# Residual update and transposes at the norm between two blocks, pass order, and a written issue order, in a two-layer decoder trunk

## Chip, cores and metric

The kernel runs on one core of a Trainium2 chip. The metric is the device time of one execution in microseconds (us); three executions of the kernel before gave 572.90, 573.61 and 573.81, with a median of 573.61. One further execution was profiled. All durations below come from it.

## The reference

Two layers act on x (256 tokens by 1024 features, float32). Each layer does:

```
h = rms_norm(x) * g_pre_mix
parts = h @ w_in                      # 1024 x 2840
mix = concat(nsa(parts), fox(parts)) @ w_out
x = x + rms_norm(mix) * g_post_mix
h = rms_norm(x) * g_pre_mlp
y = square(relu(h @ w_up)) @ w_down   # 1024 x 4096, 4096 x 1024
x = x + rms_norm(y) * g_post_mlp
```

`rms_norm(v)` is v times 1/sqrt(mean(v*v) + 1e-6), row by row. The two attention mixers (8 heads each) lie between `w_in` and `w_out`; the change leaves them as they are. What counts here are the three places where one block's result goes through a post-norm into x, and x goes through the next pre-norm into the next block's first product: mixer to MLP in layer 0, MLP of layer 0 to the mixer of layer 1, and mixer to MLP in layer 1. They are called the three junctions below. The end of layer 1 has a post-norm and a store, and no next norm.

## The kernel before

**Data layout.** The 256 tokens are two tiles t = 0, 1 of 128 tokens. Tokens lie on the partitions in `X[t]` (128 x 1024). A product with a weight needs the left operand turned, with features on the partitions: that is `xT`, 8 blocks k of 128 features by 256 tokens.

**High and low parts.** TensorE is used in its fp32r type. Each float32 operand is split into a high part (ScalarE copies it to fp32r: `whi`, `xT[0]`) and a low part (VectorE subtracts the high part from the value: `wlo`, `xT[1]`). A product is then three passes that accumulate in one PSUM bank, in `mm3`: high x high, high x low of the weight, low of x x high of the weight. Some weights get their low part through an accumulating DMA of GpSimd's queue instead, and the products with `w_down` are combined in blocks so that seven products serve for eight; neither is changed.

**A junction.** For token tile t the product leaves two PSUM banks `acc[0]`, `acc[1]` of 512 features. The function `sandwich` does, in three steps separated by `yield`: (1) ScalarE squares both banks with row sums; VectorE multiplies each bank by the product of both gains, `g_post * g_next` (tiles `mg`); seven tiny operations (`rsqrt_sum`) make the factor r of the row; VectorE makes `xg = mg * r + xo` in four pieces of 256, where `xo = x * g_next` was made ahead by `pre_gain`. (2) `to_xT` turns each half of `xg` with four 128 x 128 transposes on TensorE into one PSUM bank, ScalarE makes the high part of 128 x 512 in one instruction and VectorE the low part in one. (3) VectorE multiplies the banks once more, by `g_post` alone (tiles `m`), and adds `m * r` into X in pieces of 512. The row factor of the next norm is not in `xT`: it is applied later, to the next product or through the epsilon of the following norm.

`pre_gain` needs three multiplications of 128 x 1024 per junction, and `load_gains` brings two gain rows, spread over the partitions (512 KB each), into the buffers `gain0` and `gain1`.

**What sets the order.** All operations are first recorded, in the order of the code, by the class `Recorder`; an operation's number is its place in that record (5200 operations). A planner (`order`, `schedule`) then gives each engine its order from costs, due times, a list of overridden ranks (`RANKS`) and a mark `hot` on junction operations (`urgent`). Each engine works through its own instructions in that order: PE (TensorE), DVE (VectorE), ACT (ScalarE), POOL (GpSimd) and SP (SyncE, which issues most of the DMAs). The order between engines is kept only by waits on what an instruction reads and overwrites. Weight loads use nine rotating buffers (`raw`), so a load waits on SP until the splits of the load nine places earlier are done, and everything behind it in SP's queue waits with it.

**What follows a junction.** After the mixer, `up0` forms 512 columns of h @ w_up for t = 0 and then t = 1; after the MLP of layer 0, `in_chunk(0, evac0, by_token=True)` forms 512 columns of h @ w_in, again by tile. Both go through k = 0 to 7 and make all three passes of one k before the next. While the junction of tile 0 is worked on, PE has the products of tile 1 (`out_last`, `down`); while that of tile 1 is worked on, it has the first products of tile 0.

In the profile nearly all lines bear the number L481 (where `emit` issues everything), so operations are told apart by their tiles: `mg`, `m`, `xo`, `gains`, `xT`, `s<-cst,mg` (the transposes of xg, against the identity in `cst`), `pcs` (the scaled scores of the compressed attention branch, split in high and low, transposed against `identr`).

Of the kernel before, what the change touches and what calls it, by code (L numbers as in the profile page):

```python
# [24 lines left out]
P = 128  # L25
D = 1024
S = 256
NT = 2
# [6 lines left out]
LANE = 0.9  # L35
PASSES = 4
LANDING = 3500.0

ADDING, ADDED, CAST = 2600, (5000, 5000), (1870, 2500)
SLACK, LATE = {"vector": 20, "scalar": 20}, 1000  # L40

RAMP = {0: 900, 1: 420}
WAIT = 0.4
WARM = (256, 256, 256, 256, 128)
ENTER, LEAVE = 90, 200
SEQ = [(2, 0), (2, 1), (2, 2), (2, 3), (3, 0), (3, 1), (3, 2), (3, 3)]
EVKEY = 1
FIRSTS = [(k, k + 1) for k in range(8)]
NFIRST = 768
HOLD = 150  # L50
REACH = 40
UPK = 7
TOK, WBUFS, RBUFS = 6, 7, 9
LOAD_LEAD, SPLIT_LEAD, ADD_LEAD, CAST_LEAD = 12, 1, 5, 10
# [11 lines left out]
RANKS = (  # L66
# [17 lines left out]
)  # L84
QT = (1, 1)
# [130 lines left out]
class Op:  # L216
    __slots__ = ("small", "engine", "name", "args", "kw", "key", "urgent", "cost", "deps", "succs", "bufs",
                 "missing", "ready", "start", "end", "tile", "rank")


class Recorder:
    def __init__(self, nc, tc):
        self.nc, self.tc = nc, tc
        self.ops, self.stages, self.fifo, self.key, self.hot, self.lane, self.group = [], [], {}, None, False, None, None
        self.after = None
        for e in ("tensor", "vector", "scalar", "gpsimd", "sync"):
            setattr(self, e, _Engine(self, e))
# [15 lines left out]
    def add(self, engine, name, args, kw):  # L243
        if self.group is not None:
            assert engine == "tensor"
            self.group.append((name, args, kw))
            return
        op = Op()
        op.engine, op.name, op.args, op.kw = engine, name, args, kw
        op.key = len(self.ops) if self.key is None else self.key  # L250
        if self.lane is not None and self.key is None:
            op.key = self.lane + LANE * (len(self.ops) - self.lane)
        op.urgent = self.hot
# [4 lines left out]
        op.tile = _tile(op) if engine == "tensor" else None  # L258
        op.small = engine == "tensor" and not any(v.buf.name.startswith(("whi", "wlo")) for _, v in views)
        op.cost = _cost(op, views) + SLACK.get(engine, 0)  # L260
        deps = {} if self.after is None else {self.after: -1e9}
        op.bufs = []
        for is_out, v in sorted(views, key=lambda x: x[0]):
            b, m = v.buf, v.mask()
            if b not in op.bufs:
                op.bufs.append(b)

            def against(entries):
                for o, p, q, bank in entries:
                    if o is not op and o not in deps and (  # L270
                            (bank and engine == "tensor") or
                            (p[0] < v.p[1] and v.p[0] < p[1] and (m & q).any())):
                        deps[o] = _latency(o, op)

            against(b.writes)
            entry = (op, v.p, m, is_out and b.psum and engine == "tensor")
            if is_out:
                against(b.reads)
                b.writes = [w for w in b.writes if not (
                    w[0] in deps and v.p[0] <= w[1][0] and w[1][1] <= v.p[1] and not (w[2] & ~m).any())]  # L280
                b.writes.append(entry)
            else:
                if b.psum:
                    for o, _, _, _ in b.reads:
                        if o.engine != engine and o is not op and o not in deps:
                            deps[o] = 130.0
                b.reads.append(entry)
        op.deps = deps
        for b in op.bufs:
            if not b.ops:  # L290
                self.fifo.setdefault(b.tag, []).append(b)
            b.ops += 1
        op.succs = []
        for d in deps:
            d.succs.append(op)
        self.ops.append(op)

    def deadlines(self, out):


        due, t = {}, 0.0
        for op in out:
            if op.engine == "tensor":
                due[op], t = t, t + op.cost
        taker = {}
        for q in self.fifo.values():
            for a, b in zip(q, q[q[0].bufs:]):
                taker[a] = b
        first = {}
        for op in out:  # L310
            for b in op.bufs:
                first.setdefault(b, op)
        for op in reversed(out):
            d = due.get(op, t)
            cost = op.cost + LANDING if op.engine == "sync" else op.cost
            for x in op.succs:
                if x.deps[op] > -1e8 and x in due:
                    d = min(d, due[x] - x.deps[op] - cost)
            for b in op.bufs:
                if taker.get(b) in first and first[taker[b]] in due:  # L320
                    d = min(d, due[first[taker[b]]] - (260 if b.psum else 150) - cost)
            due[op] = d
        for op in out:
            op.rank = op.key if op.engine == "tensor" else due[op]

    def order(self):

        for op in self.ops:  # L330
            op.rank = op.key
        done = 0
        for bound in self.stages + [len(self.ops)]:
            rest = self.ops[done:]
            best = None
            for first in ([op.rank for op in rest], [op.key for op in rest]):
                for op, rank in zip(rest, first):
                    op.rank = rank
                for i in range(PASSES + 1):
                    if i:  # L340
                        kept = [op.rank for op in self.ops[:done]]
                        self.deadlines(out)
                        for op, rank in zip(self.ops, kept):
                            op.rank = rank
                    out = self.schedule()
                    end = max(op.end for op in out)
                    if best is None or end < best[0]:
                        best = end, [op.rank for op in rest]
            for op, rank in zip(rest, best[1]):
                op.rank = rank  # L350
            done = bound
# [1513 lines left out]
```

## Time and profile before

| | |
|---|---|
| median of three runs | 573.61 us (572.90 to 573.81) |
| the profiled execution, from first to last instruction | 572.4 us (572.36) |
| PE busy | 564.1 us, 99% of the span, 3696 matmuls |
| DVE busy | 534.5 us, 93% |
| ACT busy | 452.4 us, 79% |
| granted TensorE clock, mean | 0.997 |
| first matmul / last matmul's end | 0.78 us / 566.03 us |

The profiled execution is 1.25 us below the median of the runs; a prediction made against its span is carried over by that difference. "Busy" joins overlapping instructions: matmuls overlap, so a busy PE can still hold short waits of its weight loads (PEld). The stages lie so: attention of layer 0 from 6 to 118 us, its junction to the MLP 118 to 131, the MLP to 281, the junction to layer 1 281 to 300, attention 300 to 400, junction 400 to 414, MLP to 566, and then the last norm and the store.

### The profile page before, as it was taken

Reading aid. Unit: us, or ns where it says so; the run is one execution under the profiler, and the core shown is the slowest. Engines: PE = TensorE matmul, PEld = TensorE weight load, DVE = VectorE, ACT = ScalarE, POOL = GpSimd, SP = SyncE. Lnnn points to the kernel's source line nnn. Section 1 sums busy time; section 2 is a strip of 40 time slices with the busy share of each in tenths; the row PEclk is TensorE's granted clock in tenths of the full one; section 3 lists DMA queues with packets and bytes.
Section 4 is the critical chain, followed back from the end, with each engine's and each line's share of the span. In section 5 each row is a group of like instructions: output and inputs, shape, how many; then the busy total and the mean of one; then the engine's idle time right before and its main releaser. Section 6 shows DMA issues by size and latency. Waiting matters only on the chain.

```text
span 572.4 us, 10587 instructions
## 1 busy us (share of the span) xinstructions
PE 564.1 (99%) x3696; PEld 503.0 (88%) x3696; DVE 534.5 (93%) x1138; ACT 452.4 (79%) x850; POOL 49.4 (9%) x76
## 2 busy tenths in 40 slices
PE   9999999999999999999999999999999999999995
PEld 7988888789999999999889888878899999999994
DVE  7889899989999999999897899997999999999997
ACT  7898888778987877777569969986879877878873
POOL 0000200011010111000000012000111111111000
PEclk9999999999999999999999999999999999999998
DMA  8988737749999899798438685585498989888621
GB/s 322 380 307 288 272 118 237 261 155 275 289 265 289 252 253 318 196 322 229 143 109 289 251 270 156 182 279 192 142 325 238 299 251 279 259 277 257 144 38 74
DMA packets 39430, 135.69 MB, mean 237 GB/s; under 512 B 4657, under 2 KB 4817, under 8 KB 39377
## 3 DMA queue, kind: packets, MB, share of 16 engines
q1 hardware_dynamic: 31456, 106.17, 52.6%
q0 software_dynamic: 7920, 28.84, 23.0%
q8 instruction: 29, 0.48, 0.3%
q14 instruction: 25, 0.20, 0.1%
HBM read 133.92 MB, written 1.07 MB: 236 GB/s over the span
## 4 chain that ended last, share of the span: by engine, by line
PE 93%; DVE 4%; DMA 1%; ACT 1%; issue 0%; DVEq 0%; ACTq 0%
PE s L481 41%; PE acc L481 21%; PE x L481 20%; PE o L481 11%; DMA wraw<-in_w_in_dram 1%; DVE wlo L481 1%; DVE qS L481 0%; DVE m L481 0%; ACT whi L481 0%; DVE pr L481 0%; DVE x L481 0%; DVE rsqrt L481 0%; ACT qT L481 0%; DVE cs L481 0%; DVE gz L481 0%
## 5 line engine op out<-in xcount | busy, mean ns | idle before, releaser
L481 DVE TENSOR_TENSOR wlo<-wraw,whi 128x1024 fp32r<-128x1024 f32 (+2 forms) x156 | 171.9, 1108 | 10.3 <-ACT whi L481 6.2
L481 ACT ACTIVATE whi<-wraw 128x1024 fp32r<-128x1024 f32 (+2 forms) x165 | 157.9, 966 | 27.9 <-PE s L481 15.6
L481 PE MATMUL s<-xT,whi 128*128 128x256 f32 (+1 forms) x832 | 110.0, 283 | 0.0
L481 PEld LDWEIGHTS s<-xT,whi 128*128 128x128 f32 x832 | 105.2, 192 | 4.5 <-ACT y L481 0.3
L481 ACT ACTIVATE whi<-wsum 128x1024 fp32r<-128x1024 f32 x52 | 54.6, 1056 | 14.4 <-DVE wsum L481 6.0
L481 DVE TENSOR_TENSOR wlo<-wsum,whi 128x1024 fp32r<-128x1024 f32 x52 | 63.2, 1221 | 0.7 <-PE s L481 0.4
L481 PE MATMUL s<-xT,wlo 128*128 128x256 f32 x448 | 59.6, 275 | 0.0
L481 PEld LDWEIGHTS s<-xT,wlo 128*128 128x128 f32 x448 | 56.9, 192 | 1.6
L481 PE MATMUL x<-whi,aS 128*128 128x512 f32 x128 | 47.6, 379 | 0.0
L481 ACT ACTIVATE pr<-pr,st 128x256 f32<-128x256 f32 (+1 forms) x96 | 42.8, 450 | 3.7 <-DVE st L481 3.6
L481 PE MATMUL acc<-whi,aS 128*128 128x512 f32 x128 | 44.7, 380 | 0.0
L481 POOL DMA_DIRECT2D wlo<-in_w_up_dram x31 | 26.8, 865 | 150.9 <-ACT wlo L481 108.5
L481 DVE TENSOR_TENSOR wsum<-wraw,wsum 128x512 f32<-128x512 f32 x52 | 35.7, 686 | 0.1
L481 PE MATMUL s<-whi,aS 128*128 128x512 f32 x104 | 35.4, 380 | 0.0
L481 PE MATMUL acc<-whi,xT 128*128 128x512 f32 (+1 forms) x128 | 35.0, 341 | 0.0
L481 PE MATMUL x<-whi,xT 128*128 128x512 f32 x112 | 34.5, 390 | 0.0
L481 ACT ACTIVATE aS<-quads 128x896 fp32r<-128x896 f32 (+3 forms) x31 | 27.5, 891 | 8.7 <-DVE quads L481 8.2
L481 PE MATMUL acc<-xT,whi 128*128 128x512 f32 x128 | 33.0, 386 | 0.0
L481 DVE TENSOR_TENSOR aS<-quads,aS 128x896 fp32r<-128x896 f32 (+3 forms) x31 | 31.5, 1016 | 0.6 <-ACT aS L481 0.5
L481 DVE TENSOR_TENSOR wsum<-wraw 128x1024 f32<-128x1024 f32 x26 | 31.7, 1220 | 0.0
L481 POOL DMA_DIRECT2D whi<-in_w_up_dram x22 | 12.7, 576 | 203.1 <-PE s L481 71.8
L481 DVE TENSOR_TENSOR quads<-quads 128x128 f32<-128x128 f32 (+1 forms) x81 | 26.8, 335 | 1.2 <-ACT quads L481 0.8
(257 smaller groups left out, 1251.5 us busy)
## 6 DMA issues: line engine op xcount, KB each, us to landing
wraw<-in_w_down_dram SPq DMA_DIRECT2D x64, 512.0 KB, 5.7
wraw<-in_w_up_dram SPq DMA_DIRECT2D x42, 512.0 KB, 5.6
wraw<-in_w_in_dram SPq DMA_DIRECT2D x35, 512.0 KB, 5.2
wlo<-in_w_up_dram POOLq DMA_DIRECT2D x31, 512.0 KB, 7.0
whi<-in_w_up_dram POOLq DMA_DIRECT2D x22, 512.0 KB, 5.3
wraw<-in_w_out_dram SPq DMA_DIRECT2D x16, 512.0 KB, 3.7
w<-in_cmp_w_k_dram SPq DMA_DIRECT2D x8, 512.0 KB, 6.1
w<-in_cmp_w_v_dram SPq DMA_DIRECT2D x8, 512.0 KB, 5.6
```

Of the source, the lines that this page charges most:

```text
L481: getattr(getattr(self.nc, op.engine), name)(*[real(v) for v in args], **{k: real(v) for k, v in kw.items()})
```

## The change

Four things are changed, and all three junctions get them.

1. `sandwich` updates X first: `m = acc * g_post`, then `X = m * r + X` in four pieces of 256. `to_xT` turns X itself. `pre_gain`, `xg`, `xo`, the second multiplication by a gain and the later update of X are gone.
2. The next norm's gains are applied after the turn, where features lie on the partitions and a gain is one number per partition. `to_xT` does that inside the split, 128 columns at a time: four ScalarE copies with a scale instead of one of 512, and four VectorE operations `(value * gain) - high` instead of one subtraction of 512. The gains come as 16 more columns in the small `w2` load; the second gain row is not loaded. The step that turns tile t moves behind the update of X.
3. `halves_first`: the first product after a junction makes, for k = 0 to 3, the two passes with the high part of x, then for the same k the pass with its low part, and then the same for k = 4 to 7. The number of matmuls stays.
4. The planner, its costs and `RANKS` are gone. `ISSUE` is a table of the numbers of all 5236 operations (two characters each, to the base of 91) in the order in which they are issued. The table does not hold the planner's order: engine by engine, most operations stand at another place than before, in the attention and MLP stages too.

The record grows by 36: per junction, 16 more operations for the finer splits and updates (8 per tile), one DMA and three multiplications fewer.

```diff
-UPK = 7
+UPK = 14
...
-RANKS = (
...
+ISSUE = (
+    "!,!!!-!#!.!$!%!&!(!)!*#a#v!4!U!5!8!7!9!V!/!W!Z!X$)!+$8!6!Y!^!;!_![!]!0!c!d!f!:!`!a!<!=!e!b!h!k!g!l!i!?!n!>!j!A"
...
+PLACES = "".join(chr(c) for c in range(33, 127) if chr(c) not in "\"\\'")
...
+        n = len(PLACES)
+        issue = [n * PLACES.index(a) + PLACES.index(b) for a, b in zip(ISSUE[::2], ISSUE[1::2])]
+        assert sorted(issue) == list(range(len(self.ops)))
+        return [self.ops[i] for i in issue]
...
-    def load_gains(*rows):
-        g = [None, None]
-        for i, (name, l) in enumerate(rows):
-            g[i] = tile([P, D], F32, name="gains", tag=f"gain{i}")
-            nc.sync.dma_start(g[i], A[name][l].partition_broadcast(P))
+    def load_gain(name, l):
+        g = tile([P, D], F32, name="gains", tag="gain0")
+        nc.sync.dma_start(g, A[name][l].partition_broadcast(P))
         return g
...
-        w2t = small([P, 560], "w2", 1)
-        nc.sync.dma_start(w2t[:, :550], A["w2"][l])
+        w2t = small([P, 568], "w2", 1)
+        nc.sync.dma_start(w2t[:, :566], A["w2"][l])
...
+    def mm3(ps, a, b, start, stop, check=True, passes=(0, 1, 2)):
 
         ps, b = in_turns(ps), [turns(x) for x in b]
-        for j, (u, v) in enumerate(((0, 0), (0, 1), (1, 0))):
+        for j in passes:
+            u, v = ((0, 0), (0, 1), (1, 0))[j]
...
+    def halves_first():
+
+        return [(k, x) for n in (0, 4) for x in ((0, 1), (2,)) for k in range(n, n + 4)]
...
-    def to_xT(t, n, xg, xT):
+    def to_xT(t, n, g, xT):
 
         ps = psum("s")
         with nc.stretch():
             for k in range(4):
-                nc.tensor.transpose(ps[:, k * P:k * P + P], xg[:, k * P:k * P + P], ident)
-        split(ps.rearrange("p (k n) -> p k n", k=4), [y[:, 4 * n:4 * n + 4, t * P:t * P + P] for y in xT[:2]])
-
-    def pre_gain(g_post, g_next):
-
-        xo = []
-        for t in range(NT):
-            xo.append(tile([P, D], F32, name="xo", tag="fT", bufs=2))
-            nc.vector.tensor_mul(xo[t], X[t], g_next)
-        nc.vector.tensor_mul(g_next, g_next, g_post)
-        return g_next, xo
+                nc.tensor.transpose(ps[:, k * P:k * P + P], X[t][:, n * 512 + k * P:n * 512 + k * P + P], ident)
+        into = [[z[:, 4 * n + k, t * P:t * P + P] for z in xT[:2]] for k in range(4)]
+        cols = [(ps[:, k * P:k * P + P], g[:, 4 * n + k:4 * n + k + 1]) for k in range(4)]
+        for (i, c), (hi, _) in zip(cols, into):
+            nc.scalar.activation(hi, i, AF.Copy, scale=c)
+        for (i, c), (hi, lo) in zip(cols, into):
+            nc.vector.scalar_tensor_tensor(lo, i, c, hi.bitcast(F32), op0=OP.mult, op1=OP.subtract)
...
+                for a in (0, 256) if xT else (slice(0, 512),):
+                    a = slice(a, a + 256) if xT else a
+                    x = X[t][:, half(n)][:, a]
+                    nc.vector.scalar_tensor_tensor(x, m[n][:, a], r, x, op0=OP.mult, op1=OP.add)
...
         yield
+        if xT:
+            for n in range(2):
+                to_xT(t, n, g_next, xT)
+            yield
...
+        gains_mlp = par["smT"][:, 38:46]
...
-                    g_post, g_pre2 = load_gains(("g_post_mix", l), ("g_pre_mlp", l))
+                    g_post = load_gain("g_post_mix", l)
...
-        pre = pre_gain(g_post, g_pre2)
...
-            products(0, ps0, UPK, 8)
+            products(0, ps0, UPK, 16)
             square(0, ps0)
-            next(steps[0])
-            next(steps[1])
             ps1 = psum("o")
-            products(1, ps1, 0, 4)
+            products(1, ps1, 0, 8)
             turn(0)
-            products(1, ps1, 4, 8)
+            products(1, ps1, 8, 16)
```

More of the change, by code (lines that the diff above doesn't have):

```diff
@@ L10 @@
-import collections
-import heapq
 from contextlib import ExitStack, contextmanager
@@ L216 @@
 class Op:
-    __slots__ = ("small", "engine", "name", "args", "kw", "key", "urgent", "cost", "deps", "succs", "bufs",
-                 "missing", "ready", "start", "end", "tile", "rank")
+    __slots__ = ("engine", "name", "args", "kw", "bufs")
 class Recorder:
@@ L223, in __init__ @@
         self.nc, self.tc = nc, tc
-        self.ops, self.stages, self.fifo, self.key, self.hot, self.lane, self.group = [], [], {}, None, False, None, None
-        self.after = None
+        self.ops, self.group = [], None
         for e in ("tensor", "vector", "scalar", "gpsimd", "sync"):
@@ L248, in add @@
         op = Op()
[L249 to L253, printed above, removed]
+        op.engine, op.name, op.args, op.kw, op.bufs = engine, name, args, kw, []
         views = []
@@ L257, in add @@
             views += [(i in ("out", "accum_out"), v) for i, v in k.items() if isinstance(v, View)]
[L258 to L295, printed above, removed]
-        self.ops.append(op)
[L298 to L324, printed above, removed]
@@ L326, in order @@
-    def order(self):
[L330 to L351, printed above, removed]
-        for i, rank in RANKS:
-            self.ops[i].rank = rank
-        return self.schedule()
@@ L512, in _product @@
-def _product(name, args, side):
-    n = int(np.prod(args[0].shape[1:]))
-    rounded = args[1].dtype == F32R
-    if rounded and name != "transpose" and args[2].shape[-1] == 2:
-        return max(112.0, n / 2.4 + 3)
-    if name == "transpose":
-        return 85.0 if rounded else 109.0
-    if side > 1:
-        return n / 2.4 + 20 if rounded else n / 0.6 + (60 if n >= 256 else 11)
-    return max(118.0, n / 2.4 + (14 if n > 256 else 13)) if rounded else max(220.0, n / 0.6 + 7)
-def _cost(op, views):
-    out = op.args[0] if op.args else op.kw["out"]
-    n = int(np.prod(out.shape[1:]))
-    part = 100 * (out.shape[0] < P)
-    if op.engine == "gpsimd":
-        return 200 + 0.72 * n + 10 * int(np.prod(out.shape[1:-1]))
-    if op.engine == "sync":
-        v = views[0][1]
-        run = int(np.prod(v.shape[1:])) * 4 * (1.3 if v.buf.name in ("x0", "x1", "bias") else 1.0)
-        return v.shape[0] * run / 360.0
-    if op.engine == "tensor":
-        if op.name == "stretch":
-            side = P // min(op.tile)
-            return sum(_product(*x[:2], side) for x in op.args[2][::side])
-        return _product(op.name, op.args, 1)
-    if op.engine == "vector":
-        if op.name == "reciprocal":
-            return 60 + 6.5 * n
-        if op.name == "tensor_reduce":
-            n = int(np.prod(op.args[1].shape[1:]))
-        fast = op.name in ("tensor_copy", "tensor_scalar", "memset") and not any(v.buf.psum for _, v in views)
-        aps = sum(isinstance(v, View) for v in op.args[2:4]) if op.name == "tensor_scalar" else int(
-            op.name == "scalar_tensor_tensor" and isinstance(op.args[2], View))
-        return 68 + part + 64 * aps + n * (0.52 if fast else 1.04) + 10 * (op.name == "tensor_tensor_reduce")
-    src = op.args[1]
-    aps = sum(isinstance(op.kw.get(k), View) for k in ("bias", "scale", "accum_out"))
-    return n / 1.2 + (55 if src.buf.psum else 92) + 93 * aps
@@ L567, in get @@
     def get(self, i):
-        nc, marks = self.nc, self.marks
-        assert len(marks) == i
-        marks.append(len(nc.ops))
+        nc = self.nc
         kind, shape, src = self.units[i]
         if kind == "cast":
-            nc.key = marks[max(i - CAST_LEAD, 0)]
             up = i in self.ups
@@ L761, in trunk @@
         W.raw[k] = f[:, None, o + S:o + NFIRST]
-    nc.after = nc.ops[-1]
     def load_rest():
@@ L768, in trunk @@
     load_rest()
-    nc.after = None
     warm = nc.nc.const_aps.tensor(0.0, [P, S])
@@ L976, in trunk @@
         first = l == 0
-        if not first:
-            nc.stages.append(len(nc.ops))
         if first:
@@ L1242, in in_chunk, with piece @@
             parts = parts_of(l, c)
-            begin = len(nc.ops)
             ps = [None, None]
             ws = {}
-            def piece(t, k, hi, lo, k0):
-                if k == 0:
+            def piece(t, k, hi, lo, k0, passes=(0, 1, 2)):
+                if k == 0 and 0 in passes:
                     ps[t] = psum("o" if by_token and t == 0 else "x" if c in (0, 2) else "acc")
                 mm3(ps[t][:, :n], [y[:, k, t * P:t * P + P] for y in xT[:2]], (hi[:, k - k0, :], lo[:, k - k0, :]),
-                    k == 0, k == 7)
+                    k == 0, k == 7, passes=passes)
             if by_token:
                 for t in range(NT):
-                    for q, (k0, k1) in enumerate(parts):
-                        if t == 0:
-                            ws[q] = weight(l, "in", c, q)
-                        for k in range(k0, k1):
-                            piece(t, k, *ws[q], k0)
+                    for k, x in halves_first():
+                        if k // 2 not in ws:
+                            ws[k // 2] = weight(l, "in", c, k // 2)
+                        piece(t, k, *ws[k // 2], k // 2 * 2, x)
+                        if 2 in x:
                             yield
@@ L1528, in trunk @@
         if first:
-            nc.after = nc.ops[-1]
             for t in range(NT):
@@ L1532, in trunk @@
                     nc.sync.dma_start(X[t][:, half(n)], xin[t][:, half(n)])
-            nc.after = None
-        nc.lane = len(nc.ops)
         for i in range(len(flat) + 4):
@@ L1581, in urgent @@
         def urgent(gen):
-            nc.hot = True
             next(gen)
-            nc.hot = False
-        steps = [sandwich(t, [accs[t, 0], accs[t, 1]], g_post, pre, xT) for t in range(NT)]
+        steps = [sandwich(t, [accs[t, 0], accs[t, 1]], g_post, gains_mlp, xT) for t in range(NT)]
         out_last(0, 0)
@@ L1593, in trunk @@
         urgent(steps[1])
-        nc.stages.append(len(nc.ops))
         last_l = l == DEPTH - 1
@@ L1676, in up0, with products @@
             q = [None, None]
-            def products(t, ps, k0, k1):
-                for k in range(k0, k1):
+            def products(t, ps, a, b):
+                for k, x in halves_first()[a:b]:
                     if ws[k // 2] is None:
@@ L1682, in products @@
                     w = ws[k // 2]
-                    mm3(ps, [y[:, k, t * P:t * P + P] for y in xT[:2]], [y[:, k % 2, :] for y in w], k == 0, k == 7)
+                    mm3(ps, [y[:, k, t * P:t * P + P] for y in xT[:2]], [y[:, k % 2, :] for y in w], k == 0, k == 7,
+                        passes=x)
             def square(t, ps):
```

318 lines of the change are left out of this document (116 added, 202 removed), and 17 rows, old and new, of the table RANKS.

## Prediction

> **What bounds the kernel now.** I read the page's busy shares first, then the busy time by stages, then the waits, then the rows around each wait.
>
> ```profile
> span 572.4 us, 10587 instructions
> PE 564.1 (99%) x3696; PEld 503.0 (88%) x3696; DVE 534.5 (93%) x1138; ACT 452.4 (79%) x850; POOL 49.4 (9%) x76
> ```
>
> TensorE is busy for all but 8.3 us of the span. The stages say where these lie, and how full the others are (each row: window, its length, busy time of each engine).
>
> ```profile
> core 0: us, PE busy (x) PEld busy (x) DVE busy (x) ACT busy (x) POOL busy (x), PEclk, DMA share, GB/s
> 0.00:6.40 6.40, 5.62 (x15) 4.49 (x16) 2.42 (x10) 2.82 (x5) 0.20 (x4) 1.00 0.69 228
> 6.40:117.60 111.20, 110.05 (x751) 92.99 (x750) 102.60 (x331) 92.33 (x239) 4.14 (x9) 1.00 0.78 274
> 117.60:131.00 13.40, 13.40 (x72) 11.77 (x71) 12.06 (x29) 11.19 (x22) 1.45 (x2) 1.00 0.51 169
> 131.00:281.00 150.00, 150.00 (x1010) 140.27 (x1009) 145.26 (x191) 117.83 (x153) 16.51 (x22) 1.00 0.90 262
> 281.00:300.00 19.00, 19.00 (x102) 16.82 (x101) 17.48 (x37) 12.52 (x27) 0.00 (x0) 1.00 0.34 100
> 400.00:414.00 14.00, 14.00 (x74) 12.31 (x73) 13.36 (x28) 11.08 (x20) 1.44 (x2) 1.00 0.48 146
> 566.03:572.36 6.33, 0.00 (x0) 0.00 (x0) 3.16 (x8) 1.30 (x6) 1.27 (x1) 0.76 0.44 166
> ```
>
> The idle time is 6.40 - 5.62 = 0.78 at the start, 111.20 - 110.05 = 1.15 in layer 0's attention, and 6.33 behind the last matmul: 8.26. In the three junctions (117.6 to 131, 281 to 300, 400 to 414) TensorE is busy all the time. A chain that runs there on VectorE and ScalarE ends before TensorE asks for it. What can still be won is the 1.15 and the waits that hide inside "busy", since matmuls overlap:
>
> ```profile
> PE s L481 <- DVE pcs L481: 1.2, 1, 1.2
> PEld s L481 <- ACT pr L481: 0.9, 4, 0.3
> PEld acc L481 <- DVE fqT L481: 0.5, 2, 0.3
> PEld s L481 <- ACT absz L481: 0.4, 1, 0.4
> PEld s L481 <- ACT prX L481: 0.3, 1, 0.3
> PEld s L481 <- ACT y L481: 0.3, 1, 0.3
> PEld x L481 <- ACT xT L481: 0.2, 1, 0.2
> ```
>
> Beside `pcs`, the weight loads wait 0.9 + 0.5 + 0.4 + 0.3 + 0.3 + 0.2 = 2.6 us for a named tile. The `xT` of a junction is not among the large ones. TensorE's rate on its main product, by the chain of waits, is 3.45 / 16 = 0.216 us for each 512 columns:
>
> ```profile
> 118.69 3.45 PE acc L481 x16
> ```
>
> **The change part by part.** Matmuls: the transposes and passes keep their number (3696), and with it TensorE's pure work: 0.
>
> VectorE and ScalarE, by these groups (busy us, mean ns):
>
> ```profile
> L481 DVE TENSOR_TENSOR xo<-x,gains 128x1024 f32<-128x1024 f32 x6 | 7.3, 1215 | 0.6 <-PE s L481 0.6
> L481 DVE TENSOR_TENSOR gains<-gains 128x1024 f32<-128x1024 f32 x3 | 3.7, 1218 | 0.0
> L481 DVE TENSOR_TENSOR mg<-x,gains 128x512 f32<-128x512 f32 x6 | 4.2, 692 | 7.1 <-ACT rl L481 7.0
> L481 DVE TENSOR_TENSOR mg<-acc,gains 128x512 f32<-128x512 f32 x6 | 4.1, 683 | 0.3 <-ACT rl L481 0.3
> L481 DVE SCALAR_TENSOR_TENSOR x<-m,rsqrt,x 128x512 f32<-128x512 f32 x15 | 10.9, 747 | 0.1
> L481 DVE SCALAR_TENSOR_TENSOR mg<-mg,rsqrt,xo 128x256 f32<-128x256 f32 x24 | 10.1, 481 | 0.2
> L481 DVE TENSOR_TENSOR xT<-s,xT 128x512 fp32r<-128x512 f32 x12 | 8.2, 688 | 0.3
> L481 ACT ACTIVATE xT<-s 128x512 fp32r<-128x512 f32 x12 | 7.2, 596 | 4.9 <-PE s L481 4.8
> ...
> L481 ACT ACTIVATE vS<-x,rsqrt x3: 360/360/391, 20.9 to 306.5; 128x128 f32<-128x128 f32 x3
> ```
>
> Removed from VectorE: `xo` 7.3, `gains` 3.7, the second multiplication by a gain (`mg`, 4.2 + 4.1), and 12 of the updates of X in pieces of 512, 12 x 0.747 = 9.0: together 28.3. The 24 pieces of 256 that made `xg` stay as pieces of X's update (0.481 each). Added: four operations of 128 columns for one of 512 in each of 12 halves. The trace has no such operation of 128; by the slope between 512 and 256, (747 - 481) / 256 = 1.04 ns a column, it is 481 - 133 = 348 ns, so 4 x 0.348 - 0.688 = +0.70 a half, +8.4 in all. VectorE: -28.3 + 8.4 = -19.9 us. Bounds for the new one: at least a quarter of 688 (then +0), at most the 481 of 256 columns (+14.8); VectorE is relieved in each case. ScalarE: the row for a scaled 128 x 128 copy out of PSUM says 360 ns, so 4 x 0.360 - 0.596 = +0.84 a half, four halves to a junction: +3.4 in each, +10.1 in all.
>
> The Trainium skill (VectorE: DVE Perf Modes, "The TRN2 errata — SBUF-src ops pay a fixed extra latency per instruction") speaks against this split: the cost above the columns is fixed for each instruction, so work should stay in pieces of 512 or more. By its ScalarE formula for PSUM sources (172 cycles plus the columns at 1.2 GHz) I estimate 4 x 0.25 - 0.57 = +0.43 a half, or 1.7 a junction; the rows ask twice that, and I go by the rows.
>
> In time these two edits give nothing, since nothing in a junction holds TensorE: 0 for VectorE's relief. The 3.4 of ScalarE a junction has this cover: 11.19 + 3.4 = 14.6 of 13.4 us in the first (1.2 too much), 12.52 + 3.4 = 15.9 of 19.0, 11.08 + 3.4 = 14.5 of 14.0 (0.5 too much). The excess is weight splits that slip into the next stage, where ScalarE has 150.00 - 117.83 = 32 us free. I take 0, and 1.2 + 0.5 = 1.7 if the splits are needed at once.
>
> Pass order. Before, tile 0's first half went thus in the first junction:
>
> ```profile
> 122.62 0.60 ACT L481 ACTIVATE xT<-s 128x512 fp32r<-128x512 f32 x1
> 123.25 0.69 DVE L481 TENSOR_TENSOR xT<-s,xT 128x512 fp32r<-128x512 f32 x1
> 123.86 1.22 DVE L481 TENSOR_TENSOR wlo<-wraw,whi 128x1024 fp32r<-128x1024 f32 x1
> ...
> 124.07 0.46 PE L481 MATMUL s<-whi,xT 128*128 128x512 f32 x1
> ```
>
> The first pass with the low part came two matmuls, 0.43 us, behind the first with the high part; after, eight matmuls, 1.73 us. Into these 1.73 VectorE must bring its first low part, for which it needs 0.35, and the split that the table puts ahead of it, 1.22: 1.57, in time by 0.2. With a multiplication by the gain (0.69) ahead as well it would be late by 0.5. I take 0; bounds -0 (nothing waits there now) and +0.5 for each of 6 tiles at most, if all meet it.
>
> DMA. The rows of the first junction's gains, of the split that frees a weight buffer, of a later weight load, and of the first use:
>
> ```profile
> 87.95 0.33 SPq L481 DMA_DIRECT2D gains<-in_g_post_mix_dram  x1
> DMA to landing us min/median/max: 4.9/5.7/6.4
> 111.92 1.22 DVE L481 TENSOR_TENSOR wlo<-wraw,whi 128x1024 fp32r<-128x1024 f32 x1
> 118.37 0.69 DVE L481 TENSOR_TENSOR mg<-x,gains 128x512 f32<-128x512 f32 x1 [1.99 <-ACT rl L481]
> ```
>
> In the table this load stands nine places later in SP's queue (69th instead of 60th), behind a weight load whose buffer comes free with the split that ran at 111.92. The table puts that split about 6 us of VectorE's work earlier, at some 106, so it ends at 107, the gains go out at about 107.5 and land by 113.9, 4.5 before 118.4: 0. The second gain row (a load of 512 KB, three times) goes. The other small loads that are moved (`w2` of layer 1 by 21 places, its `bias` by 96) are needed only 200 us later.
>
> The table elsewhere. The largest wait is this (the matmul row's bracket is the idle time in front):
>
> ```profile
> 63.49 0.76 DVE L481 TENSOR_SCALAR pr<-pr,st,gate 128x256 f32<-128x256 f32 x2
> 64.16 0.97 DVE L481 TENSOR_TENSOR pcs<-cs,pcs 128x256 fp32r<-128x256 f32 x2
> 64.86 0.36 PE L481 MATMUL s<-identr,pcs 128*128 128x128 f32 x2 [1.15 <-DVE pcs L481]
> ```
>
> In the table the two scalings of `pr` (0.76) stand behind the two subtractions of `pcs`. Counting everything ahead of `pcs`, VectorE has 1.08 us less and TensorE 0.43 us less in front: the wait shrinks by 1.08 - 0.43 = 0.65. Late next is `pr`, at 0.76 later, and TensorE has other attention products between. Bounds: 0 (something else ends last) to -1.15. The other named waits, 2.6, fall on operations nearly all of which have moved: of TensorE's 3139 recorded operations 2810 stand at another place. A new order that opens no new wait could take all (-2.6), one as good as the old takes 0; I take -0.8, about a third, because they are small waits of 0.2 to 0.4 that a shift by one matmul (0.216) halves. Start: same loads, one warm-up product placed later, 0 (0.2 either way). End: same instructions behind the last matmul, 0.
>
> Sum: -0.65 - 0.8 = -1.45, rounded to -1.5: 572.36 - 1.5 = 570.9 span, and 1.25 more since the median of the runs stands so much above it (573.61 - 572.36): **572.1 us**.
>
> **The rivals.**
>
> *ScalarE becomes late in the junctions (slower).* The 1.2 and 0.5 us that do not fit are then weight splits that the products behind the junction wait for. It decides from the point where a split's lead is under 1.2 us. For it: 11.19 of 13.4 is already full; against it: no wait of TensorE for `whi` or `wlo` is in the list, so splits run ahead. With the small waits unchanged: 573.6 + 1.7 = 575.3. By the skill's figure, 1.7 instead of 3.4 a junction, there would be no excess in the first (12.9 of 13.4), and this rival would be nothing.
>
> *Gains late (slower).* If the split at 111.92 keeps its time, it ends at 113.1, and the gains go out after that, at the latest where a later load went (115.43): in the middle at 114.3, landed by 120.7, 2.3 behind 118.4. The junction's chain has 124.07 - 123.22 = 0.85 to spare (the high part's end against its first matmul), so TensorE waits 1.4: 573.6 + 1.4 = 575.0. Against it: the split's place, 6 us earlier by the count.
>
> *As many waits as before (no change).* TensorE was full, VectorE's 19.9 us are hidden, and the table opens as many small waits as it closes: 573.6. For it: 564.1 of the span is pure work; against it: the order in front of `pcs` is shorter by its count.
>
> *All named waits go (faster by more).* 572.36 - 1.15 - 2.6 = 568.6, run 569.9. For it: one order fixed as a whole can place each of them; against it: the `pcs` chain has only 0.65 to give by the count.
>
> **How the numbers follow.** Forecast 0.44 (572.1), all waits go 0.10 (569.9), no change 0.30 (573.6), late ScalarE 0.10 (575.3), late gains 0.06 (574.7). A measurement tells 0.2%, 1.15 us, from no change. Faster: 0.44 + 0.10 = 0.54, same 0.30, slower 0.16. The range: below to 570.0, where the last wait goes; above to 575.2, which takes in no change, late gains and nearly all of the excess on ScalarE. The forecast's own range is 571.0 to 573.0.
>
> **What would show it.** Right: the wait on `pcs` at 64.86 falls to about 0.5; the last matmul ends near 564.5; the junctions' windows stay 100% busy on TensorE; `xo`, `mg` and the product of gains are gone from the groups, 48 copies `xT<-s` of 128x128 on ScalarE near 0.36 and 48 on VectorE near 0.35; VectorE's busy time near 515, ScalarE's near 462. Wrong: new waits of TensorE on `whi`, `wlo`, `xT` or `m` behind a junction; a wait of VectorE on the gains' DMA near 118; TensorE's busy time no less than 564 with named waits of 2.6 us or more beside `pcs`.

## The result, and the profile after

The changed kernel takes 577.97 us (median of four runs, 577.68 to 580.98), the kernel before 573.25 in the runs beside it: a ratio of 1.0095, 95% interval 1.0070 to 1.0119. The change makes the kernel 4.7 us slower; 572.1 had been forecast, with 570.0 to 575.2 as the range.

Every run of this study lists its span beside its time, and the time is 1.7 to 1.85 us above the span in all of them (the profiled execution after: 578.09 with 576.3). By this the profiled execution before, 572.36, belongs to a run of about 574.1, above the four runs of before that stand beside the change (up to 573.81) and 0.9 above their median; the 1.25 us with which the prediction carried its span over to the median was not that difference. In the first run below one of five executions was slow (590.79, granted clock 0.948); without it that run's median of 577.80 is 577.69.

The page after, its first line and its busy times:

```profile
span 576.3 us, 10603 instructions
PE 565.9 (98%) x3696; PEld 501.6 (87%) x3696; DVE 521.3 (90%) x1141; ACT 459.2 (80%) x886; POOL 50.7 (9%) x76
```

VectorE is busy 13.2 us less than before, ScalarE 6.8 more, and TensorE has the same 3696 matmuls. The stages (window, length, busy time of each engine, as in the prediction's table):

```profile
60.00:110.00 50.00, 49.51 (x341) 40.45 (x340) 48.45 (x185) 43.61 (x132) 5.22 (x9) 1.00 0.63 215
110.00:118.00 8.00, 7.45 (x48) 5.71 (x47) 5.16 (x11) 3.05 (x6) 0.57 (x1) 1.00 0.91 287
118.00:132.00 14.00, 14.00 (x75) 12.28 (x74) 12.45 (x37) 11.77 (x31) 0.88 (x1) 1.00 0.46 113
132.00:282.00 150.00, 148.84 (x1001) 138.65 (x1000) 135.47 (x181) 117.87 (x154) 16.62 (x22) 1.00 0.86 254
282.00:301.00 19.00, 19.00 (x102) 16.79 (x101) 17.54 (x54) 15.72 (x47) 0.00 (x0) 1.00 0.48 149
402.00:416.00 14.00, 14.00 (x74) 12.30 (x73) 12.80 (x37) 12.74 (x33) 1.41 (x2) 1.00 0.46 134
416.00:565.00 149.00, 148.31 (x969) 137.31 (x968) 140.21 (x190) 118.15 (x154) 18.15 (x24) 1.00 0.78 226
570.00:576.30 6.30, 0.00 (x0) 0.00 (x0) 3.00 (x7) 1.14 (x5) 1.24 (x1) 0.69 0.44 166
```

In the three junctions TensorE is busy all the time, as before. The new idle time lies outside: in the attention of layer 0 and in both MLPs. The waits of TensorE after:

```profile
PE acc L337 <- ACT aS L337: 0.7, 1, 0.7
PE s L337 <- ACT rl L337: 0.7, 1, 0.7
PE x L337 <- DVE oT L337: 0.6, 1, 0.6
PE s L337 <- DVE pr L337: 0.5, 1, 0.5
PE s L337 <- ACT quads L337: 0.5, 1, 0.5
```

These are five waits, none of which before had, and the one for `pcs` is gone. The rows count only the time in which no matmul is still running. Taken from one matmul's start to the next, less what the same pair takes elsewhere ("from start to start" below), the five cost 0.86 (`aS`, at 426), 0.85 (`rl`, 250), 0.71 (`oT`, 116), 0.65 (`pr`, 89) and 0.64 with 0.14 just behind it (`quads`, 139): 3.85 us. Two of them read row by row:

```profile
86.60 2.57 DVE L337 TENSOR_TENSOR wlo<-wraw,whi 128x1024 fp32r<-128x1024 f32 x1
86.59 2.85 POOL L337 TENSOR_SCALAR_AFFINE_SELECT bias<-bias 128x256 f32<-128x256 f32 x5
89.85 0.30 PE L337 MATMUL s<-cst,pr 128*128 128x128 f32 x1 [0.49 <-DVE pr L337]
...
115.48 1.22 DVE L337 TENSOR_TENSOR wsum<-wraw 128x1024 f32<-128x1024 f32 x1 [2.62 <-DMA wraw<-in_w_down_dram]
116.63 0.68 DVE L337 TENSOR_TENSOR oT<-o,oT 128x512 fp32r<-128x512 f32 x1
117.36 0.48 PE L337 MATMUL x<-whi,oT 128*128 128x512 f32 x1 [0.55 <-DVE oT L337]
```

At 86.6 the table has GpSimd make five mask selects in a row, which before came in pairs between 61 and 69; a VectorE subtraction beside them takes 2.57 us where its group's mean was 1.22, and the scaling of `pr` queued behind it is late. At 112.9 VectorE stands 2.62 us for a weight transfer, because the table has moved a sum of weight blocks there that before ran at 132.5; the low part of `oT` is queued behind it. The other three are of this second kind, an order that is wrong for what TensorE needs next: at 250 a weight split stands ahead of `rl` on ScalarE, and at 139 and 426 TensorE's own order asks for a tile too soon behind the transposes that start it.

### The profile page after: what moved, and what is told of

It reads as the page before. It is cut to its first block, busy times and chain, and to the rows that moved or that the text cites. A ratio compares the mean times of both kernels' runs of the same rounds, so it can differ in the third digit from the quotient of the medians.

```text
span 576.3 us, 10603 instructions
## 1 busy us (share of the span) xinstructions
PE 565.9 (98%) x3696; PEld 501.6 (87%) x3696; DVE 521.3 (90%) x1141; ACT 459.2 (80%) x886; POOL 50.7 (9%) x76
## 4 chain that ended last, share of the span: by engine, by line
PE 92%; DVE 3%; DMA 2%; ACT 2%; issue 1%; DVEq 0%; SPq 0%
PE s L337 41%; PE acc L337 23%; PE x L337 19%; PE o L337 10%; DMA wraw<-in_w_down_dram 1%; ACT whi L337 1%; DMA first<-in_first_dram 1%; DVE wlo L337 0%; DVE m L337 0%; DVE pr L337 0%; DVE x L337 0%; DVE qS L337 0%; DVE wsum L337 0%; ACT wlo L337 0%; DVE gz L337 0%
## 5 line engine op out<-in xcount | busy, mean ns | idle before, releaser
L337 ACT ACTIVATE whi<-wraw 128x1024 fp32r<-128x1024 f32 (+2 forms) x165 | 155.8, 964 | 12.9 <-PE x L337 4.0
L337 PE MATMUL s<-xT,whi 128*128 128x256 f32 (+1 forms) x832 | 131.8, 284 | 0.7 <-ACT rl L337 0.7
L337 PEld LDWEIGHTS s<-xT,whi 128*128 128x128 f32 x832 | 121.0, 191 | 8.0 <-ACT rl L337 1.4
L337 PE MATMUL s<-xT,wlo 128*128 128x256 f32 x448 | 72.8, 274 | 0.0
L337 PEld LDWEIGHTS s<-xT,wlo 128*128 128x128 f32 x448 | 66.8, 191 | 3.5
L337 PE MATMUL acc<-whi,aS 128*128 128x512 f32 x128 | 45.9, 381 | 0.7 <-ACT aS L337 0.7
L337 PE MATMUL s<-whi,aS 128*128 128x512 f32 x104 | 38.7, 380 | 0.0
L337 PE MATMUL acc<-xT,whi 128*128 128x512 f32 x128 | 36.6, 396 | 0.1
L337 ACT ACTIVATE wlo<-whi 128x1024 fp32r<-128x1024 f32 x23 | 24.2, 1051 | 8.1 <-PE x L337 3.0
```

The lines of the kernel that those rows point to most:

```text
L337: getattr(getattr(self.nc, op.engine), name)(*[real(v) for v in args], **{k: real(v) for k, v in kw.items()})
```

## Experiments

Theory O at first: the edits in the junctions cost nothing, the loss is the table's order. Theory E: the edits cost it. It turned out that both hold, in different orders.

**The edits in the old order.** The change's table was replaced by the order of before, the new operations at the places of those they stand for; in the second run with the change's pass order.

```diff
-ISSUE = (the change's table)
+ISSUE = (the order of before; xg's instructions -> X's, one copy -> four, one subtraction -> four)
```

> The three junctions as in the change (X updated first and turned, gains applied per partition in pieces of 128, one gain row loaded), but every operation at the place that the planner of before gave it, new operations at the place of those they stand for, and the three passes of one k together as before. Only the small load of layer 1's w2 and two small copies that read it had to go behind the first junction. Theory O (the loss of 4.7 us lies in the issue order outside the junctions): the edits cost nothing, 572.5 to 574, VectorE's busy time near 514 us, TensorE's junction windows without a wait. Theory E (the edits themselves cost it: ScalarE's and VectorE's finer pieces come late): 576 or more, with TensorE waiting in the junctions or right behind them.

> The same, and in the six first products behind the junctions the passes in the order of the change (high parts of k 0 to 3, then the low part of these, then k 4 to 7). Theory O: as the run without it, within 0.5 us, since the low part's wait was not what held TensorE. Theory E: some us above before, if the pass order is what makes the low parts late; below the other run, if the pass order pays for the finer pieces.

Measured: 577.80, ratio 1.0079 (1.0065 to 1.0092), and 578.52, 1.0093 (1.0079 to 1.0106). Theory O fell: the edits cost 4.5 us in the old order, and the pass order doesn't win any of it back. The waits of TensorE in the second:

```profile
PE o L337 <- DVE wlo L337: 1.5, 1, 1.5
PE s L337 <- DVE h L337: 1.5, 2, 0.9
PE s L337 <- DVE x L337: 0.7, 2, 0.5
```

These stand in or right behind the junctions: transposes of X at 128 and 412, a weight's low part at 294, the first `h` behind a junction at 134 and 420. Two more of 0.2 us lie elsewhere. From start to start all seven come to 5.4 us, which is what the run loses (5.2).

**The table mended.** Five places outside the junctions, then the first of them alone.

```diff
-GpSimd:  load of w_up, five selects        (both layers)
+GpSimd:  five selects, load of w_up
-VectorE: wsum, oT
+VectorE: oT, wsum
-TensorE: h transposes apart from their pair (139, 426)
+TensorE: h transposes behind their pair
-ScalarE: weight split, quads (139); weight split, rl (250)
+ScalarE: quads, weight split; rl, weight split
```

> The changed kernel with five places of its table mended, outside the junctions: GpSimd's weight load behind the mask selects (both layers), VectorE's sum of two weight blocks behind the low part of oT, two transposes of h and ScalarE's copy of them earlier, ScalarE's relu of one product ahead of a weight split, two other transposes earlier. In the changed kernel's profile TensorE's next matmul came 0.65, 0.71, 0.64 and 0.14, 0.85 and 0.86 us late at these five places, 3.85 in all. Theory O: about 3.8 us faster than the changed kernel, 574.2 (573.5 to 575). Theory E: unchanged, 577 to 578.

> The changed kernel with only the first of these mended: GpSimd's mask selects no longer wait behind a weight load and run some 20 us earlier, not as a burst of five at 86.6. If GpSimd's selects slow VectorE while both run (theory O says so: the split at 86.60 took 2.57 us instead of 1.22, and the scaling of pr that waits behind it made TensorE late by 0.65): that split takes 1.2 us and the wait before the transposes of pr is gone, some 0.6 us faster, 577.3; but the selects then run near VectorE's work at 66, where a slowdown may come back. Otherwise (the split was slow for another reason): the split stays at 2.5 us, and the time at 578.

Measured: 575.82, ratio 1.0053 (1.0036 to 1.0069), so 2.2 us faster than the change, not 3.8; and 577.71, 1.0084 (1.0067 to 1.0101), no difference from the change that can be told. In the second the subtraction is whole again:

```profile
86.82 1.22 DVE L337 TENSOR_TENSOR wlo<-wraw,whi 128x1024 fp32r<-128x1024 f32 x1
...
PE s L337 <- ACT rl L337: 1.6, 2, 0.9
PE x L337 <- DVE gcol L337: 0.6, 1, 0.6
```

The wait at 89 is gone, but TensorE now waits twice for `rl` (218 and 472), and 0.6 for another tile at the start. With all five mended others come up too:

```profile
PE s L337 <- ACT q_tok L337: 0.7, 1, 0.7
PE s L337 <- ACT quads L337: 0.3, 1, 0.3
PE x L337 <- DVE gcol L337: 0.2, 1, 0.2
PE s L337 <- DVE kx L337: 0.2, 1, 0.2
```

From start to start the waits for `q_tok`, `quads` and `kx` cost 0.80, 0.41 and 0.33; the place of `gcol`, at the start, costs 0.69 and cost 0.64 in the change too. So of 3.85 some 1.5 come back, which leaves 2.3, near the 2.2 measured.

**What in the edits is dear.** Theory P: the pieces of 128. Theory X: X first. Whole pieces under X first, and pieces alone in the kernel before:

```diff
 # fifth run, to_xT: gains left out
-    four: activation(hi, ps_k, Copy, scale=g_k); four: (ps_k * g_k) - hi
+    split(ps of 512)                  # one copy, one subtraction
 # sixth run, to_xT of before
-    split(ps of 512)
+    four: activation(hi, ps_k, Copy); four: ps_k - hi
```

> As the first run (the junctions of the change at the places of the order of before), but the split of each turned half in one copy of 512 and one subtraction of 512, as before, in place of four and four of 128. The next norm's gains are left out of the computation (a gain per partition can't be applied in one instruction of 512). The first run came out at 577.8, with TensorE waiting in and behind the junctions, which theory O had not said. Theory P (the pieces of 128 make the junction late: four copies at a pitch of 0.26 us take 1.1 us instead of 0.6, the low parts as much): 573 to 574, junctions without a wait. Theory X (updating X first makes it late, the pieces don't matter): 577 or more.

> The kernel before in its own order, fixed as a list, with one thing changed: the split of each turned half in four copies and four subtractions of 128, at the places of the one copy and the one subtraction of 512. X is still updated last, the gains still go through the products. Theory P: about 4 us slower than before, 576 to 578, with waits of TensorE for the transposes or low parts in the junctions. Theory X: 573.3, no change.

Measured: 573.05, ratio 1.0002 (0.9991 to 1.0012): X first costs nothing that can be told. And 573.98, 1.0015 (1.0006 to 1.0025): plain pieces cost some 0.6 us, not 4. Neither theory was right alone; what differed from the first run was the gain column. So the same two kernels the other way round:

```diff
 # ninth run, to_xT of before: pieces with a column of ones
+    four: activation(hi, ps_k, Copy, scale=ones); four: (ps_k * ones) - hi
 # tenth run, X first: plain pieces, gains left out
+    four: activation(hi, ps_k, Copy); four: ps_k - hi
```

> The kernel before in its own order, fixed as a list, with the split of each turned half in four copies and four subtractions of 128, each multiplied by a column of the partitions as in the change; the column holds ones, so nothing else changes. In the sixth run plain pieces (no column) cost 0.6 us only: four plain copies took 0.79 us, four scaled ones of the second run 1.14, one whole copy 0.60. Theory S (the column makes the pieces dear, and the junctions have no room for it): 576.5 to 578, as in the first run, although X is updated last. Theory XS (only pieces and X first together are late): 574 to 574.5.

> The first run's kernel (X first, order of before) with plain pieces of 128: four copies without a scale and four plain subtractions. The next norm's gains are left out of the computation. Theory S: about 573.7, 0.6 above the run with whole pieces (573.05) and 4 below the first run (577.8). Theory XS: 576 or more.

Measured: 577.75, ratio 1.0086 (1.0073 to 1.0100), and 573.40, 1.0008 (0.9999 to 1.0018). All in the order of before, in us:

| pieces | X last (before) | X first |
|---|---|---|
| whole, 512 | 573.3 | 573.05 |
| 128, plain | 573.98 | 573.40 |
| 128, with a column | 577.75 | 577.80 |

The upper left figure is that of the runs of before beside them (573.0 to 573.4), and the two upper kernels on the right leave the next norm's gains out. The column is the price, whichever way X is updated. With it and X last (ninth run) TensorE waits at the same places as in the second run, for the transposes of xg (`mg`) and for `h`:

```profile
PE s L585 <- DVE h L585: 1.3, 2, 0.7
PE s L585 <- DVE mg L585: 0.9, 3, 0.5
```

The groups of plain pieces (sixth run) and of pieces with a column (ninth), busy us and mean ns:

```profile
L585 DVE TENSOR_TENSOR xT<-s,xT 128x128 fp32r<-128x128 f32 x48 | 10.3, 281 | 0.5 <-ACT xT L585 0.5
L585 ACT ACTIVATE xT<-s 128x128 fp32r<-128x128 f32 x48 | 9.3, 294 | 3.7 <-PE s L585 3.5
```
```profile
L585 ACT ACTIVATE xT<-s,one 128x128 fp32r<-128x128 f32 x48 | 13.4, 382 | 3.6 <-PE s L585 3.6
L585 DVE SCALAR_TENSOR_TENSOR xT<-s,one,xT 128x128 fp32r<-128x128 f32 x48 | 13.2, 343 | 1.6 <-ACT xT L585 1.6
```

And how it reaches the chain, in the first half of the first junction: plain (sixth run), then with a column (second run):

```profile
122.39 0.79 ACT L585 ACTIVATE xT<-s 128x128 fp32r<-128x128 f32 x4
123.21 0.89 DVE L585 TENSOR_TENSOR xT<-s,xT 128x128 fp32r<-128x128 f32 x4 [0.23 <-ACT xT L585]
```
```profile
122.03 1.14 ACT L337 ACTIVATE xT<-s,w 128x128 fp32r<-128x128 f32 x4
123.21 1.12 DVE L337 SCALAR_TENSOR_TENSOR xT<-s,w,xT 128x128 fp32r<-128x128 f32 x4 [0.59 <-ACT xT L337]
```

From the first copy to the last low part: 123.21 + 0.89 - 122.39 = 1.71 us plain, 2.30 with a column, 123.25 + 0.69 - 122.62 = 1.32 whole (before). Plain pieces add 0.39 a half, and the junctions nearly have room for that (0.6 us in the whole kernel); for another 0.59 they don't (3.8 us more).

**The wait for `pcs`.** The one gain of the prediction that had a count behind it, alone in the kernel before; and the kernel before a second time.

```diff
 # seventh run, order of before
-VectorE: gz, pr, pr, pcs, pcs
+VectorE: pcs, pcs, pr, pr, gz
-TensorE: pcs transposes, pr, pcs, k products, ..., three products
+TensorE: three products, pcs transposes, k products, pr
 # twelfth run: nothing
```

> The kernel before in its own order, fixed as a list, with the one wait of 1.15 us in layer 0's attention mended: VectorE scales pr (two instructions) and makes one small product behind the two subtractions of pcs, TensorE takes three products ahead of the transposes of pcs and the transposes of pr behind them, ScalarE copies pr's transposes behind those of pcs. Nothing of the junctions is changed. If the wait before pcs is worth its length: some 0.9 us faster than before, 572.4, the wait at 64.86 gone. If what was behind it only becomes late in its turn: 573.3, with a new wait for pr or its products between 65 and 70.

> The kernel before with its own order written out as a list: the same instructions in the same order, as a second look at it. The profiled execution of before had 572.4 us and a wait of 1.15 for pcs; the seventh run, which takes that wait away, was no faster in its timed runs (573.5 against 573.4) though its last matmul ended at 564.8 instead of 566.0. If the wait is in every execution of before: it is there again, 1.0 to 1.2, last matmul near 566. If it comes and goes (VectorE's subtractions of pcs share their time with GpSimd's selects, whose start hangs on a transfer): shorter or absent, with a span near 571.5, and then it was never worth 0.65 in the median.

Measured: 573.53, ratio 1.0007 (0.9997 to 1.0018), and 573.39, 1.0007 (0.9997 to 1.0018). The second profiled execution of before:

```profile
span 570.5 us, 10587 instructions
PE 563.4 (99%) x3696; PEld 501.6 (88%) x3696; DVE 534.2 (94%) x1138; ACT 452.3 (79%) x850; POOL 51.4 (9%) x76
...
62.48 0.75 DVE L584 TENSOR_TENSOR pcs<-cs,pcs 128x256 fp32r<-128x256 f32 x2
63.28 0.29 PE L584 MATMUL s<-identr,pcs 128*128 128x128 f32 x2
```

The order is the same, there is no wait, and the span is 1.9 us shorter. ScalarE tells why, by its waits for transfers and by the split of one weight, in the first profiled execution and in the second:

```profile
ACT whi L481 <- DMA wraw<-in_w_in_dram: 2.8, 3, 2.2
...
57.63 1.06 ACT L481 ACTIVATE whi<-wraw 128x1024 fp32r<-128x1024 f32 x1 [2.17 <-DMA wraw<-in_w_in_dram]
```
```profile
ACT whi L584 <- DMA wraw<-in_w_in_dram: 0.5, 2, 0.4
...
55.44 1.06 ACT L584 ACTIVATE whi<-wraw 128x1024 fp32r<-128x1024 f32 x1
```

In the execution that the prediction read, a weight landed 2.2 us later. Its load went out at the same time in both (51.2 and 51.1) and took 6.4 us instead of 4.3 to land; ScalarE and VectorE ran 2 us behind from there, and `pcs` was where TensorE met it. Two other runs with this order of the attention bear it out: where ScalarE waited 1.87 (sixth run) and 1.09 (second) for this weight, TensorE waited 0.97 and 0.23 for `pcs`.

**The table in the junctions only.** The order of before outside, the table in windows round the junctions; first narrow, then wider and mended.

```diff
-ISSUE = (order of before everywhere)
+ISSUE = (table in 116-134, 280-304, 398-418)                              # eighth run
+ISSUE = (table in 110-146, 274-312, 394-432; waits at 116, 139, 426 mended) # eleventh
```

> The change's computation with the order of before, except in three windows round the junctions (116 to 134, 280 to 304, 398 to 418 us), where all engines follow the table. The five waits that the table brought outside are not in it. If the table's worth is that it hides the finer pieces in the junctions, and its loss lies outside (theory O for the table, P for the pieces): 573 to 574, no wait of TensorE in the junctions, which the second run (578.5, order of before everywhere) had. If the loss in the junctions is there in any order: 577 or more.

> The change's computation in the order of before, except in three wider windows (110 to 146, 274 to 312, 394 to 432 us), where all engines follow the table; of the table's waits in these windows those at 116, 139, 140.5 and 426 are mended. In the eighth run (576.8) TensorE waited 1.8 us each for h and for its copies, in front of the transposes of h at 131.7 and 415.9, just behind the narrower windows: the table puts these transposes 4 and 3 us later. If the table's order of junction and first products behind it is what makes room for the scaled pieces: 573.3 to 574.3, no such waits. If they come back elsewhere: 576 or more.

Measured: 576.83, ratio 1.0065 (1.0052 to 1.0078), and 573.82, 1.0018 (1.0008 to 1.0028). In the narrow one the waits moved to its rear edge:

```profile
PE s L337 <- DVE h L337: 1.8, 1, 1.8
PE s L337 <- ACT quads L337: 1.6, 1, 1.6
```

With the first products behind the junction in the table's order as well, they are gone, and the change's computation is 4.1 us faster than in its own table, 0.18% behind before. Of that rest of 0.8 to 1.0 us, 0.7 from start to start is one new wait, for `aS` at 150:

```profile
PE acc L337 <- ACT aS L337: 0.6, 1, 0.6
```

No version run here beats before.

**How often TensorE's long products are interrupted.** Against the second profiled execution of before, which is among the shortest of its runs, the change's span is 5.8 us longer, and 3.85 of named waits don't fill that; 1.3 remain when the gap of 0.64 in front of the change's first product, at 4.65, is taken off too. Counted in the matmul records, transposes and short products stand in 89 groups among the long products before, in 120 after.

```diff
 # thirteenth run, order of before, at 68 places of TensorE's queue
-transpose, transpose, product, product
+transpose, product, transpose, product
```

> The kernel before in its own order as a list, with only TensorE's order changed: at 68 places, where several transposes or short products stand in a row, one of the long products that follow them is taken in between. Before has 89 groups of transposes and short products among the long ones, the changed kernel 120, this one 157. Set against the second look at before (span 570.5), the changed kernel's named waits leave 1.3 us over, that is 0.042 us for each of its 31 more groups. Theory I (each group costs TensorE some time of its own): 68 x 0.042 = 2.9 us slower than before, 576, without named waits to that amount. Otherwise: 573.3 plus only what the named waits of TensorE in its profile come to.

Measured: 578.10, ratio 1.0088 (1.0075 to 1.0102), 5.0 us slower. Its waits:

```profile
span 576.6 us, 10585 instructions
...
PE s L584 <- ACT prT L584: 0.8, 2, 0.6
PE s L584 <- ACT quads L584: 0.7, 2, 0.4
PE s L584 <- DVE gs L584: 0.5, 1, 0.5
PE x L584 <- ACT xT L584: 0.4, 1, 0.4
PE s L584 <- ACT pcT L584: 0.2, 1, 0.2
```

By these rows the named waits are 2.6. But they leave out the time in which the matmul ahead is still running; from start to start, the measure used for the change's 3.85, the seven cost 4.1 (0.68 at 4.9, 0.61 at 42, 0.82 at 66, 0.61 at 142, 0.34 at 352, 0.47 at 353, 0.61 at 425). What is left, 5.0 - 4.1 = 0.9 by the medians or 6.1 - 4.1 = 2.0 by the spans, is 0.013 to 0.029 us for each of 68 groups; for the change's 31 that makes 0.4 to 0.9 us. Theory I had 2.9 us without named waits and gets a third to two thirds of it: most of this run's loss is waits that the new order opened, and the price of an interruption as such is small at most. Whether what is left is the switch itself or waits too short for the table of waits isn't told apart.

## Why the prediction was wrong

- **What bounds the kernel**: right. TensorE's work is the time, and each version's time is, to about 1 us, that work plus the waits its order leaves (from start to start 5.4 for 5.2 us lost in the second run, 4.0 for 3.5 in the eighth, 3.8 for 4.8 in the ninth, 4.1 for 5.0 in the thirteenth).
- **VectorE and ScalarE in the junctions at 0**: right for the change (TensorE busy 14.00 of 14.00, 19.00 of 19.00, 14.00 of 14.00), for a reason that the step didn't give. It took ScalarE's 32 free us of the next stage as the cover. The cover is the table's order in and behind the junction (eighth and eleventh run). Among other moves it spreads the first four transposes of `h`: in layer 0 they come 4.0 to 4.3 us behind the last turn of the junction before, 3.8, 6.2, 7.8 and 8.5 behind it after; this move wasn't tried alone. In the order of before the same edits cost 4.5 us, though ScalarE needs less than was counted (four scaled copies take 1.14 us for one whole of 0.60, +0.54 a half against +0.84, since following copies overlap). A busy total per window can't tell this: the length of the chain counts. That TensorE never waits in a window says only that the chain fits, not by how much.
- **VectorE relieved by 19.9**: its busy time fell by 13.2. The step added single durations, and in the trace the durations of neighbours overlap (four low parts of 0.34 us take 1.12). Nothing hung on it.
- **ScalarE late in the junctions**, a rival at 0.10: not what the change met. In the old order the junctions did become late, but by 4.5 us and not 1.7, and TensorE's waits there are for tiles that VectorE writes (`wlo`, `h`, `x`); ScalarE's own share in them isn't told apart.
- **Gains late**: did not come. The load went out at 109.38 instead of 107.5 and `m` at 119.33 didn't wait for it. (The rival's time is 575.0 where it is worked out, and 574.7 beside its chance; the sum gives 575.0.)
- **Pass order at 0**: right within 0.7 in the order of before (578.52 beside 577.80, intervals overlap).
- **`pcs`, -0.65**: the wait is gone after, but before doesn't have it either in its second profiled execution, and mending it alone won nothing (seventh run). The step took the order ahead of `pcs` for the cause, and the cause was a late transfer. A term read from one execution needs its releaser followed to the end, and the row of ScalarE's wait for `w_in` (2.2 us) was there to follow.
- **The table elsewhere, -0.8**: the step that failed. Its bounds were 0 and -2.6: it allowed that moved operations open as many waits as they close, but not more, and no reason excluded a loss. The runs showed 3.85 us of new waits instead of 0.8 saved; with the 0.4 to 0.9 that the thirteenth run allows for interruptions that is 4.3 to 4.8, against 4.7 measured. GpSimd's queue was not looked at; one of the five waits came from there. With TensorE full before, an order of 5200 places could hardly win and could lose in each of them: that asymmetry belonged in the bounds.
- **TensorE's pure work at 0**: right in the number of matmuls. A price of their order beside the named waits is at most the 0.4 to 0.9 us above; it isn't shown apart from short waits.

## What to carry to other kernels

When the limiting engine is already full, read a rewritten issue order for what it can open: for each engine, GpSimd's queue included, look for a wait on a transfer, or work that isn't urgent, ahead of what the full engine needs next. Measure the slack of a chain before lengthening it, since a little extra work (0.39 us a half) can be nearly free and a little more (another 0.59) can cost 3.8 us. Count every wait in one measure, from one start to the next on the full engine: the seven idle stretches of the thirteenth run add up to 2.6 us and cost 4.1. Take a second execution of the same kernel before counting on a wait that occurs once.

## What was not expected of the hardware

- A column operand has its own price: ScalarE's copy of 128 columns out of PSUM took 294 ns plain and 382 with a scale per partition, VectorE's low part 281 and 343. The Trainium skill (ScalarE: Activation LUTs, "What ACT_TABLE_LOAD costs") states 186 ns plus 0.833 ns a column with constants, about 93 ns more for each operand of one value per partition, and that neighbours overlap by about 93. By it I estimate 293 and 386 ns, and the runs agree; the overlap was larger here, about 129 ns (four in 0.79 us plain and in 1.14 with a scale). The prediction used the scaled row, but never asked what of it was the scale.
- VectorE and GpSimd got into each other's way in one place: a subtraction of 1024 columns took 2.57 us instead of 1.22 beside five selects in a row, and 1.22 again in the fourth run, where the selects ran elsewhere. The Trainium skill (GPSIMD Engine Reference, "1. Specifications") says that the two share an interface to SBUF and contend when VectorE reads two inputs there, which this subtraction does; the trace agrees.
- One more group of transposes among long products cost at most 0.013 to 0.029 us beside the waits that the order opened (thirteenth run).
